# Sixteen experts on one core: rows of tokens by indirect DMA, a scatter matrix by comparison, and weights of two experts in one tile of 8 KB runs

## The chip, the cores and the metric

The kernel runs on one core of a Trainium2 chip: TensorE (PE; weight loads PEld), VectorE (DVE), ScalarE (ACT), GpSimd (POOL), and SyncE (SP), which here only issues transfers. Sixteen DMA engines move data between HBM and the on-chip memory. The metric is the device time of one execution in microseconds.

## What is computed

Two blocks of two layers each over 512 tokens of width 1024. The first block is attention and does not change. Each layer of the second block ends in a mixture of 16 experts, in which every expert takes the 64 tokens that score highest for it:

```python
def _ec_moe(h, router, w1, w3, w2):
    cap = EC_CAPACITY * n // N_EXPERTS          # 64
    probs = jax.nn.softmax(jnp.einsum('bnd,de->ben', h, router).astype(jnp.float32), axis=1)
    gates, idx = lax.top_k(probs, cap)
    xs = h[bidx, idx]
    a = jnp.einsum('becd,edf->becf', xs, w1)
    g = jnp.einsum('becd,edf->becf', xs, w3)
    y = jnp.einsum('becf,efd->becd', jax.nn.silu(a) * g, w2) * gates[..., None].astype(h.dtype)
    return jnp.zeros_like(h).at[bidx, idx].add(y)
```

All is fp32. One expert has three matrices of 1024 x 1024, 4 MB each; 16 experts make 201 MB a layer, each read once, and there are two such layers (0 and 1). Layer 0 follows a mixer, layer 1 a conformer.

## The kernel before

`moe(l)` (L1711) takes the experts in pairs, `p` from 0 to 7: the 64 tokens of one expert stand in columns 0 to 63 of TensorE's array, those of the other in 64 to 127. The residual `xn` is kept transposed, eight tiles of 128 features x 512 tokens; `kt` is the same, scaled, with tokens on the partitions.

**Routing.** Eight rounds of max and replace on DVE find each expert's tokens; a scan and two transposes turn that into `sT`, each token's slot in each expert.

**A pair.** `gather(p)` compares `sT` with the numbers 1 to 64 (`cst`) and gets a one-hot matrix `G` of tokens by slots. The tokens are gathered by TensorE: 32 matmuls of `kt` with `G` (L1780), four to each of eight feature chunks, whose results ACT and DVE scale and shift into `xs`. `slots` (L1788) gets the gates from `G` by four small matmuls and transposes `G` into `GT` by four more. `stage` (L1818) runs three times: `xs` by `w1`, `xs` by `w3`, and the product by `w2`; each is 32 matmuls (L1829) of 64 columns by 512, two of which, one for each expert, run side by side. An fp32 matmul runs in two passes, and the profile counts each pass, so it shows 64 in a stage and 64 in a gather; the prediction counts as the profile does. Between the second and the third the product is transposed (L1847). `scatter` (L1803) multiplies the result, split in a high and a low part, by `GT` (16 matmuls, L1807) and DVE adds the eight chunks to `xn` (L1808). The gather of pair p+1 is written after the scatter of pair p, and its chunks go between the matmuls of the first stage.

**Weights.** `load` (L1723) fetches a tile of 1 MB, 256 rows of one expert's matrix, as two runs of 4 KB in each of 128 partitions. There are 20 such tiles in turn, 12 (`mr`) and 8 (`mq`), 20 MB. 192 loads a layer stand on SP's queue in the order of use; each waits until the matmuls have done with the tile that it overwrites, and the first 20 are issued before the routing is done. Behind the last stand the conformer's first loads (L132, L134).

What sets the order is the code and a scheduler that places instructions of an engine by it; each engine runs its own list in order.

Of the kernel before, what the change touches and what calls it, by code (L numbers as in the profile page):

```python
# [22 lines left out]
KD = D // 128  # L23
# [4 lines left out]
SCRATCH = ((D, N), (2, 9, 128, 512), (1536, NT))  # L28
# [20 lines left out]
class K:  # L49
# [1510 lines left out]
    MB, MQ = 12, 8  # L1560
# [150 lines left out]
    def moe(self, l):  # L1711
# [5 lines left out]
        with self.ms, ExitStack() as es:  # L1717
            mp = es.enter_context(self.pool("moe"))
            W = (A["exp_w1"][l], A["exp_w3"][l], A["exp_w2"][l])
            todo = itertools.product(range(8), range(3), range(4), range(2))  # L1720
            order = itertools.cycle([(self.mring, "mr", self.MB)] * self.MB + [(mp, "mq", self.MQ)] * self.MQ)

            def load():  # L1723

                p, wi, kk, e = next(todo)
# [5 lines left out]
            kt = [self.t(mp, [128, D], tag=f"kt{t}") for t in range(4)]  # L1731
            gh = self.t(mp, [128, 8], tag="gh")
            sT = self.t(mp, [128, 4, E], tag="sT")
            with self.pool("mg") as gp:
                r, pr = self.route
                pt = self.bank()
                for t in range(4):
                    nc.tensor.transpose(pt[0:E, t * 128:t * 128 + 128], pr[:, t, :], self.ident[:])
                wk, cum = [self.t(gp, [E, N], tag=tag) for tag in ("wk", "cum")]
                pv = pt[0:E, :]  # L1740
                one = self.t(gp, [E, N], tag="mone")
                nc.gpsimd.memset(one[:], 1.0)

                for t in range(4):
                    for half in range(2):
                        pt = self.bank()
                        for c in range(4):
                            nc.tensor.transpose(pt[:, c * 128:c * 128 + 128], xn[4 * half + c][:, t * 128:t * 128 + 128],
                                                self.ident[:])
                        nc.scalar.activation(kt[t][:, half * 512:half * 512 + 512], pt[:], AF.Copy, scale=r[:, t:t + 1])  # L1750

                m8 = self.t(gp, [E, 8], tag="m8", bufs=2)
                for _ in range(CAP // 8):
                    nc.vector.max(m8[:], pv)  # L1754
                    nc.vector.match_replace(wk[:], m8[:], pv, -1.0)  # L1755
                    pv = wk[:]
                nc.vector.tensor_scalar(wk[:], wk[:], -1.0, None, op0=ALU.is_equal)
                nc.vector.tensor_tensor_scan(cum[:], one[:], wk[:], 0.0, op0=ALU.mult, op1=ALU.add)
                pts = []
                for x in (wk, cum):  # L1760
                    pt = self.bank()
                    for t in range(4):
                        nc.tensor.transpose(pt[:, t * 16:t * 16 + 16], x[:, t * 128:t * 128 + 128], self.ident[0:E, 0:E])
                    pts.append(pt[:, 0:64].rearrange("p (t e) -> p t e", t=4))
                nc.scalar.copy(sT[:], pts[0])
                nc.vector.tensor_tensor(sT[:], sT[:], pts[1], op=ALU.mult)
            xp = es.enter_context(self.pool("mx"))

            def gather(p):

                G = self.t(xp, [128, 512], tag="G", bufs=1)[:].rearrange("p (t n) -> p t n", t=4)
                nc.vector.tensor_tensor(G.rearrange("p t (e j) -> p t e j", e=2),  # L1772
                                        sT[:, :, 2 * p:2 * p + 2][:, :, :, None].to_broadcast([128, 4, 2, CAP]),
                                        cst[:][:, None, None, :].to_broadcast([128, 4, 2, CAP]), op=ALU.is_equal)
                xs = self.t(xp, [128, KD, 128], tag="xs", bufs=1)
                yield xs, G
                for c in range(KD):
                    px = self.bank()[:, 0:128]
                    for t in range(4):
                        mm(px, kt[t][:, c * 128:c * 128 + 128], G[:, t, :], start=t == 0, stop=t == 3)  # L1780
                    sc, sh = self.s1m[:, c:c + 1], mod[:, 24 + c, 0:1]
                    if c % 2 == 0:
                        nc.scalar.activation(xs[:, c, :], px, AF.Identity, scale=sc, bias=sh)  # L1783
                    else:
                        nc.vector.tensor_scalar(xs[:, c, :], px, sc, sh, op0=ALU.mult, op1=ALU.add)  # L1785
                    yield c

            def slots(p, G):  # L1788

                pg = self.bank()  # L1790
                for t in range(4):
                    mm(pg[:, 0:2], G[:, t, :], pr[:, t, 2 * p:2 * p + 2], start=t == 0, stop=t == 3)  # L1792
                for e in range(2):
                    es = slice(64 * e, 64 * e + 64)
                    nc.vector.tensor_scalar(gh[es, p:p + 1], pg[es, e:e + 1], 0.5, None, op0=ALU.mult)
                pb = self.bank()
                for t in range(4):
# [3 lines left out]
                return GT  # L1801

            def scatter(GT, yh, yl, st=None):  # L1803
# [8 lines left out]

            for p in range(8):
                parts = gather(p)
                xs, G = next(parts)
                next(parts)

                def stage(wi, lhs):  # L1818
                    ps = [self.bank(), self.bank()]
                    for kk in range(4):  # L1820
                        wt = []
                        for e in range(2):
                            wt.append(loaded.pop(0) if loaded else load())
                        for k2 in range(2):
                            k = 2 * kk + k2
                            next(parts, None)
                            for hf in range(2):
                                for e in range(2):
                                    mm(ps[hf][64 * e:64 * e + 64, :], lhs(k, e), wt[e][:, k2, hf * 512:hf * 512 + 512],  # L1829
                                       start=k == 0, stop=k == 7)  # L1830
                    return ps
                xl = lambda k, e: xs[:, k, 64 * e:64 * e + 64]
                pa = stage(0, xl)
# [5 lines left out]
                GT = slots(p, G)  # L1839
                pg = stage(1, xl)  # L1840
                sb = self.t(xp, [128, 8, 128], tag="xs", bufs=1)
                for hf in range(2):
# [3 lines left out]
                    for c in range(4):  # L1846
                        nc.tensor.transpose(pt[:, c * 128:c * 128 + 128], s[:, (4 * hf + c) * 128:(4 * hf + c + 1) * 128], self.ident[:])  # L1847
# [171 lines left out]
```

## Time and profile before

| | us |
|---|---|
| median of 3 runs (3161.67 to 3165.59) | 3161.85 |
| the profiled execution | 3164.56 |
| its span, first to last instruction | 3162.7 |
| TensorE busy in it | 2887.3 |
| DVE, ACT, GpSimd busy | 1503.0, 930.1, 799.7 |
| mean granted TensorE clock | 0.949 |
| expert loads (SP), `mr` and `mq` | 384 of 1024 KB |

The profile is of one execution, with times from the start of its span. Layer 0's experts run from about 1886 to 2402, layer 1's from about 2634 to 3150. A matmul's end is modelled, and neighbours overlap, so the step from one start to the next tells more than a busy time. The DMA share is the sum of all packets' times over 16 engines and can pass 1.

### The profile page before, as it was taken

Reading aid. Unit: us, or ns where it says so; the run is one execution under the profiler, and the core shown is the slowest. Engines: PE = TensorE matmul, PEld = TensorE weight load, DVE = VectorE, ACT = ScalarE, POOL = GpSimd, SP = SyncE. Lnnn points to the kernel's source line nnn. Section 1 sums busy time; section 2 is a strip of 40 time slices with the busy share of each in tenths; the row PEclk is TensorE's granted clock in tenths of the full one; section 3 lists DMA queues with packets and bytes.
Section 4 is the critical chain, followed back from the end, with each engine's and each line's share of the span. In section 5 each row is a group of like instructions: output and inputs, shape, how many; then the busy total and the mean of one; then the engine's idle time right before and its main releaser. Section 6 shows DMA issues by size and latency. Waiting matters only on the chain. (4 is left out here: it accounts for less than half of the span.)

```text
span 3162.7 us, 38266 instructions
## 1 busy us (share of the span) xinstructions
PE 2887.3 (91%) x14942; PEld 1846.0 (58%) x14942; DVE 1503.0 (48%) x2743; ACT 930.1 (29%) x1667; POOL 799.7 (25%) x669
## 2 busy tenths in 40 slices
PE   6889899998999999999998779998999998899988
PEld 3486577775688567765676754444445664444443
DVE  5886574556516555784366841112116552211122
ACT  2434344343424544344344221001002241001001
POOL 2242233422423334444344720000003330000000
PEclk8999899998899999999998889999999998999999
DMA  9631033221443134232322179999983557999993
GB/s 280 205 130 55 15 111 112 91 71 50 143 131 122 46 100 141 93 96 86 95 74 94 60 278 388 391 390 403 396 326 94 186 201 309 396 384 396 401 401 119
DMA packets 273924, 621.30 MB, mean 196 GB/s; under 512 B 15215, under 2 KB 144247, under 8 KB 273488
## 3 DMA queue, kind: packets, MB, share of 16 engines
q1 hardware_dynamic: 265568, 597.63, 52.1%
q0 software_dynamic: 4848, 17.04, 1.7%
q10 hardware_dynamic: 3328, 4.20, 0.4%
q8 instruction: 117, 1.92, 0.2%
q14 instruction: 63, 0.52, 0.1%
HBM read 603.96 MB, written 14.95 MB: 196 GB/s over the span
## 5 line engine op out<-in xcount | busy, mean ns | idle before, releaser
L154 POOL TENSOR_TENSOR wl<-ring,wh 128x512 fp32r<-128x512 f32 x304 | 418.2, 1379 | 655.0 <-ACT wh L153 636.9
L1829 PE MATMUL b<-mr,xs 128*64 128x512 f32 x1920 | 441.3, 605 | 0.0
L153 ACT CAST wh<-ring 128x512 fp32r<-128x512 f32 x304 | 186.9, 618 | 504.3 <-PE b L161 363.9
L159 PE MATMUL b<-hh,wh 128*128 128x512 f32 (+1 forms) x800 | 295.8, 371 | 3.0 <-DVE sc L621 3.0
L160 PE MATMUL b<-hh,wl 128*128 128x512 f32 (+1 forms) x800 | 291.6, 365 | 1.3 <-POOL wl L154 1.3
L161 PE MATMUL b<-hl,wh 128*128 128x512 f32 (+1 forms) x800 | 290.6, 365 | 0.1
L1829 PEld LDWEIGHTS b<-mr,xs 128*64 128x64 f32 x1920 | 143.7, 139 | 224.8 <-issue 214.7
L1829 PE MATMUL b<-mq,xs 128*64 128x512 f32 x1152 | 260.9, 600 | 0.0
L1780 PEld LDWEIGHTS b<-G,kt 128*128 128x128 f32 x1024 | 137.8, 212 | 136.1 <-issue 80.5
L1780 PE MATMUL b<-G,kt 128*128 128x128 f32 x1024 | 160.4, 309 | 52.1 <-DVE G L1772 52.1
L763 PE MATMUL av<-P,kv 128*64 128x512 f32 (+2 forms) x672 | 193.8, 522 | 2.9 <-ACT P L813 1.7
L1785 DVE TENSOR_SCALAR xs<-b,s1m,m 128x128 f32<-128x128 f32 x64 | 26.2, 409 | 322.2 <-PE b L1780 322.2
L159 PEld LDWEIGHTS b<-hh,wh 128*128 128x128 f32 x800 | 154.1, 193 | 32.3 <-issue 5.6
L160 PEld LDWEIGHTS b<-hh,wl 128*128 128x128 f32 x800 | 153.8, 192 | 27.0 <-issue 4.3
L161 PEld LDWEIGHTS b<-hl,wh 128*128 128x128 f32 x800 | 153.4, 192 | 25.1 <-issue 4.5
L1829 PEld LDWEIGHTS b<-mq,xs 128*64 128x64 f32 x1152 | 86.0, 138 | 138.0 <-issue 132.8
L813 ACT ACTIVATE P<-s 128x512 f32<-128x512 f32 (+2 forms) x224 | 116.6, 550 | 116.6 <-PE s L760 112.8
L362 PE MATMUL b<-wh,hh 128*128 128x256 f32 x512 | 148.9, 291 | 2.1 <-DVE kb L1160 1.3
L363 PE MATMUL b<-wl,hh 128*128 128x256 f32 x512 | 148.3, 290 | 0.3 <-POOL wl L154 0.3
L364 PE MATMUL b<-wh,hl 128*128 128x256 f32 x512 | 147.7, 289 | 0.4 <-DVE hl L345 0.4
L1855 DVE SCALAR_TENSOR_TENSOR yl<-b,gh,xs 128x512 fp32r<-128x512 f32 x32 | 22.6, 746 | 247.2 <-ACT xs L1854 247.2
L1783 ACT ACTIVATE xs<-b,m,s1m 128x128 f32<-128x128 f32 x64 | 29.3, 457 | 373.4 <-PE b L1780 373.4
(543 smaller groups left out, 5631.5 us busy)
## 6 DMA issues: line engine op xcount, KB each, us to landing
mr<-in_exp_w_dram SPq DMA_DIRECT2D x240, 1024.0 KB, 9.8
mq<-in_exp_w_dram SPq DMA_DIRECT2D x144, 1024.0 KB, 11.4
ring<-in_w_mod_dram SPq DMA_DIRECT2D x96, 512.0 KB, 4.2
ring<-in_w_in_dram SPq DMA_DIRECT2D x96, 512.0 KB, 3.7
ring<-in_ada_w_dram SPq DMA_DIRECT2D x48, 512.0 KB, 3.8
ring<-in_w_out_dram SPq DMA_DIRECT2D x32, 512.0 KB, 4.5
bias<-in_BS_dram POOLq DMA_DIRECT2D x16, 512.0 KB, 4.0
bias<-in_BT_dram POOLq DMA_DIRECT2D x16, 512.0 KB, 4.2
```

What stands on the lines that cost most here:

```text
L153: nc.scalar.copy(h, src)
L154: nc.gpsimd.tensor_tensor(l, src, h.bitcast(F32), op=ALU.subtract)
L159: m(out, w[0], x[0], start=start, stop=False, skip_group_check=chk)
L160: m(out, w[1], x[0], start=False, stop=False, skip_group_check=chk)
L161: m(out, w[0], x[1], start=False, stop=stop, skip_group_check=chk)
L362: m(o, hh, wh[:, kk, :], start=(k == 0 and i % 2 == 0), stop=False, skip_group_check=True)
L363: m(o, hh, wl[:, kk, :], start=False, stop=False, skip_group_check=True)
L364: m(o, hl, wh[:, kk, :], start=False, stop=stop, skip_group_check=True)
L763: mm(av[64 * i:64 * i + 64, a:b], vf(i, kt), P, start=start, stop=stop)
L813: nc.scalar.activation(p[:, :w], ps[:, :w], AF.Exp)
L1780: mm(px, kt[t][:, c * 128:c * 128 + 128], G[:, t, :], start=t == 0, stop=t == 3)
L1829: mm(ps[hf][64 * e:64 * e + 64, :], lhs(k, e), wt[e][:, k2, hf * 512:hf * 512 + 512], start=k == 0, stop=k == 7)
```

## The change

Four things are changed in `moe`, and the two constants for its tiles.

1. **Tokens.** The rows of `kt` are written to HBM scratch (`k_d`, four stores of 512 KB on ACT's queue). The slot matmul, now with four columns, also gives each slot's token number (`mnum` holds them), and GpSimd fetches the 128 rows of a pair by an indirect DMA into `xg`. TensorE transposes `xg` in eight pieces; ACT and DVE scale and shift as before. The 32 gather matmuls are gone.
2. **Scatter matrix.** `GT` is a comparison on DVE of the numbers 0 to 511 with the token numbers `gi`; the four transposes and ACT's copy are gone.
3. **Weights.** A tile is 2 MB, for both experts of a pair: 256 rows of each, and a partition holds two neighbouring rows of each, one run of 8 KB. `MB, MQ = 6, 4` keep 20 MB. 96 loads a layer. Because of that, feature k of a tile is every second one, hence `every2nd` and the scale vectors `sp1`, reordered by eight small matmuls.
4. **Order.** The scatter of pair p goes behind the first weight tile of pair p+1's first stage; the gather of pair p+1 is issued after the first stage of pair p and transposed inside its third.

The squares that close the layer go to `xg`, `xs` and one `mq` tile instead of `kt` and `G`.

```diff
-    MB, MQ = 12, 8
+    MB, MQ = 6, 4
...
-                w = self.t(pool, [128, 2, 1024], tag=tag, bufs=bufs)
-                nc.sync.dma_start(w[:], kview(W[wi][2 * p + e, kk * 256:(kk + 1) * 256, :]))
-                return w
+                w = self.t(pool, [128, 2, 2048], tag=tag, bufs=bufs)
+                nc.sync.dma_start(w[:], W[wi][2 * p:2 * p + 2, kk * 256:(kk + 1) * 256, :]
+                                  .rearrange("e (p k) n -> p e (k n)", k=2))
+                return w[:].rearrange("p e (k n) -> p e k n", k=2)
...
+                nc.scalar.dma_start(self.k_d[t * 128:t * 128 + 128, :], kt[:])
...
-                for c in range(KD):
-                    px = self.bank()[:, 0:128]
-                    for t in range(4):
-                        mm(px, kt[t][:, c * 128:c * 128 + 128], G[:, t, :], start=t == 0, stop=t == 3)
...
-                pb = self.bank()
-                for t in range(4):
-                    nc.tensor.transpose(pb[:, t * 128:t * 128 + 128], G[:, t, :], self.ident[:])
-                GT = self.t(xp, [128, N], F32R, tag="G", bufs=1)
-                nc.scalar.copy(GT[:], pb[:])
+                    mm(pg[:, 0:4], G[:, t, :], pg4[:, t, p, :], start=t == 0, stop=t == 3)
+                nc.vector.tensor_copy(ix[:, p:p + 1], pg[:, 2:3])
+                nc.vector.tensor_copy(gi[:, p:p + 1], pg[:, 2:3])
...
+                xg = self.t(xp, [128, D], tag="xg", bufs=1)
+                nc.gpsimd.indirect_dma_start(xg[:], None, self.k_d,
+                                             bass.IndirectOffsetOnAxis(ap=ix[:, p:p + 1], axis=0))
...
+                        nc.tensor.transpose(pt[:, k * 128:k * 128 + 128], every2nd(xg, k0 + k), self.ident[:])
...
+            def scatter(p, yh, yl, st=None):
+                GT = self.t(xp, [128, N], F32R, tag="GT", bufs=1)
+                nc.vector.tensor_scalar(GT[:], num[:, 0:N], gi[:, p:p + 1], None, op0=ALU.is_equal)
...
             for p in range(8):
+                xl = lambda k, e, xs=xs: xs[:, k, 64 * e:64 * e + 64]
+                pa = stage(xl, lambda kk: scatter(*late) if late and kk == 0 else None)
+                xg = gather(p + 1) if p < 7 else None
...
+                pg = stage(xl)
...
+                if p < 7:
+                    nxt = inputs(xg)
+                    xs = next(nxt)
+                py = stage(lambda k, e, sb=sb: sb[:, k, 64 * e:64 * e + 64],
+                           lambda kk: next(nxt, None) if kk in (1, 2) else None)
+                late = p, *outputs(p, py)
...
+            free = [self.t(xp, [128, D], tag=tag, bufs=1)[:] for tag in ("xg", "xs")]
+            free += [self.t(mp, [128, 4096], tag="mq", bufs=self.MQ)[:]]
```

TensorE's list where a pair's first stage begins, before: gather matmuls (`G`, `kt`) stand between the expert matmuls (`mr`).

```order
L1780 MATMUL b_16715<-G_16712,kt_3491_16105 128x128
L1780 MATMUL b_16715<-G_16712,kt_3492_16106 128x128
L1780 MATMUL b_16715<-G_16712,kt_3493_16107 128x128
L1780 MATMUL b_16715<-G_16712,kt_3494_16108 128x128
L1780 MATMUL b_16727<-G_16712,kt_3491_16105 128x128
L1780 MATMUL b_16727<-G_16712,kt_3492_16106 128x128
L1780 MATMUL b_16727<-G_16712,kt_3493_16107 128x128
L1780 MATMUL b_16727<-G_16712,kt_3494_16108 128x128
L1829 MATMUL b_16721<-mr_16723,xs_16714 64x512
L1829 MATMUL b_16721<-mr_16725,xs_16714 64x512
```

The same place after, from a third stage's last tile on: the expert matmuls of the next pair follow at once, and the scatter (`GT`) comes behind the first tile.

```order
L1859 MATMUL b_16986<-mq_17036,sb_16970 64x512 x2
L1859 MATMUL b_16987<-mq_17036,sb_16970 64x512 x2
L1859 MATMUL b_17052<-mq_17054,xs_16985 64x512 x2
L1859 MATMUL b_17053<-mq_17054,xs_16985 64x512 x2
L1859 MATMUL b_17052<-mq_17054,xs_16985 64x512 x2
L1859 MATMUL b_17053<-mq_17054,xs_16985 64x512 x2
L1844 MATMUL b_17066<-GT_17064,sb_17046 128x512
L1844 MATMUL b_17066<-GT_17064,yl_17047 128x512
```

GpSimd's list after the mixer's last split (`wl`): the number table, the copies for the slot matmul, and the gathers, in an engine that had nothing in this layer before.

```order
L154 TENSOR_TENSOR wl_15986<-ring_15967,wh_15985 128x512
L1739 DMA num_16093<-in_mnum_dram 128x516
L1773 COPY pg_3485_16092<-num_16093 128x32x2
L1772 COPY pg_3485_16092<-pr_16043 128x32x2
L1801 DMA xg_16213<-scratch,ix_16090 128x1024
L1801 DMA xg_16279<-scratch,ix_16090 128x1024
```

GpSimd now stands between the routing and the first expert matmul.

SP's list at the end of layer 0, after: the conformer's small load (`cv`) and its weights (`ring`).

```order
L182 DMA cv_3859_18069<-in_cv_dram 128x16
L132 DMA ring_18079<-in_cf_w_dram 128x4x128 x2
L132 DMA ring_18082<-in_cf_w_dram 128x4x128 x2
L134 DMA ring_18171<-in_w_mod_dram 128x4x256
L134 DMA ring_18173<-in_w_mod_dram 128x4x256
```

Before, the first two of these pairs of `ring` rows stood ahead of `cv`; now they stand behind it. The first `ring` load now waits for the squares' last sum (L317), whose operands lie where that ring tile will be; before, it waited for expert matmuls of the last pair.

## Rows read from the trace of the kernel before

**Rows 1.** waits of SP, 1900 to 2350 us: total us, times, longest.
```profile
SPq L1728 <- PE b L1829: 340.7, 85, 13.6
```

**Rows 2.** waits of TensorE's weight loads, same stretch: the one wait for a transfer.
```profile
PEld b L1829 <- DMA mr<-in_exp_w_dram: 0.2, 1, 0.2
```

**Rows 3.** busy us of each engine by stretch, then granted clock, DMA share, GB/s.
```profile
1880.00:1886.00 6.00, 1.16 (x9) 1.04 (x9) 4.74 (x10) 0.21 (x1) 0.00 (x0) 0.50 1.03 410
1960.00:1980.00 20.00, 20.00 (x108) 9.31 (x110) 2.92 (x7) 2.69 (x5) 0.00 (x0) 1.00 0.97 353
2120.00:2150.00 30.00, 25.43 (x128) 12.97 (x126) 9.14 (x14) 3.35 (x6) 0.00 (x0) 1.00 1.03 410
```

**Rows 4.** chain that ended last, one expert pair of layer 0: start, us, what.
```profile
2146.53 1.87 PE b L1829 x8
...
2169.33 13.95 PE b L1829 x64
2184.70 13.95 PE b L1829 x64
2199.46 1.44 PE b L1807 x5
2200.92 2.53 DVE xn L1808 x4
...
2206.93 3.09 PE b L1780 x16
2210.03 2.43 PE b L1829 x8
```

**Rows 5.** groups by line, layer 0, gather: busy us, mean ns, idle before.
```profile
L1780 PE MATMUL b<-G,kt 128*128 128x128 f32 x512 | 80.1, 308 | 26.0 <-DVE G L1772 26.0
```

**Rows 6.** timeline of TensorE, last pair of layer 1; columns: start, us.
```profile
3105.90 1.05 PE L1792 MATMUL b<-pr,G 128*128 128x2 f32 x8
...
3107.38 7.09 PE L1829 MATMUL b<-mq,xs 128*64 128x512 f32 x32
...
3122.75 14.01 PE L1829 MATMUL b<-mr,xs 128*64 128x512 f32 x64
```

**Rows 7.** DMA, 2120 to 2150 us, runs of 4 KB: packets, MB, share.
```profile
DMA packets 3187, 12.29 MB, mean 410 GB/s; under 512 B 190, under 2 KB 190, under 8 KB 3186
...
q1 hardware_dynamic: 3186, 12.27, 102.5%
```

**Rows 8.** DMA, 12 to 15.3 us: a load with 8 KB runs, almost alone.
```profile
DMA packets 109, 0.84 MB, mean 253 GB/s; under 512 B 7, under 2 KB 7, under 8 KB 7
...
q1 hardware_dynamic: 109, 0.84, 60.1%
```

**Rows 9.** timeline of TensorE where the first pair of layer 0 begins.
```profile
1885.99 3.76 PE L1780 MATMUL b<-G,kt 128*128 128x128 f32 x16 [1.20 <-DVE G L1772]
1889.67 2.22 PE L1829 MATMUL b<-mr,xs 128*64 128x512 f32 x8
```

**Rows 10.** timeline of SP: the first load that waited for a freed tile.
```profile
1894.87 6.79 SPq L1728 DMA_DIRECT2D mr<-in_exp_w_dram  x4
```

**Rows 11.** timeline of TensorE: first expert matmul of layer 1.
```profile
2637.49 2.07 PE L1829 MATMUL b<-mr,xs 128*64 128x512 f32 x8
```

**Rows 12.** tile bias, 512 KB loads issued by GpSimd: issue ns (min/median/max), landing.
```profile
L1023 POOL DMA_DIRECT2D bias<-in_BS_dram x16: 528/568/604, 167.6 to 1280.7; - x16
...
DMA to landing us min/median/max: 3.7/4.0/6.1
```

**Rows 13.** timeline of TensorE where layer 0 ends and the conformer begins.
```profile
2384.71 4.51 PE L1829 MATMUL b<-mr,xs 128*64 128x512 f32 x20
...
2400.97 1.05 PE L317 MATMUL b<-mean,G 128*128 128x2 f32 x8 [0.78 <-DVE G L283]
...
2408.07 0.80 PE L159 MATMUL b<-eh,wh 128*128 128x512 f32 x1 [1.59 <-ACT eh L344]
```

**Rows 14.** timeline of SP: the conformer's first weight loads.
```profile
2353.79 14.09 SPq L132 DMA_DIRECT2D ring<-in_cf_w_dram  x4
```

More of the change, by code (lines that the diff above doesn't have):

```diff
@@ L1730, in moe @@
             loaded = [load() for _ in range(self.MB + self.MQ)]
[L1731 to L1735, printed above, removed]
+            xp = es.enter_context(self.pool("mx"))
+            gh, gi = [self.t(xp, [128, 8], tag=tag) for tag in ("gh", "gi")]
+            ix = self.t(xp, [128, 8], I32, tag="ix")
@@ L1739, in moe @@
[L1739 to L1742, printed above, removed]
-                for t in range(4):
[L1745 to L1750, printed above, removed]
@@ new lines, in moe @@
+            nc.gpsimd.tensor_copy(pg4[:, :, :, 2:4], num[:, 512:516][:, :, None, None].to_broadcast([128, 4, 8, 2]))
+            pp = self.bank()
+            sp1 = self.t(xp, [128, 2, 8], tag="sp1")
+            for i, src in enumerate((self.s1m[:], mod[:, 24:32, 0])):
+                for h in range(2):
+                    for par in range(2):
+                        o = 8 * i + par
+                        mm(pp[64 * h:64 * h + 64, o:o + 7:2], self.ident[:, par:par + 127:2], src[:, h:8:2],
+                           start=True, stop=True)
@@ new lines, in inputs @@
+            def inputs(xg):
+                xs = self.t(xp, [128, KD, 128], tag="xs", bufs=1)
+                yield xs
+                for k0 in (0, 4):
+                    pt = self.bank()
+                    for k in range(4):
+                        nc.tensor.transpose(pt[:, k * 128:k * 128 + 128], every2nd(xg, k0 + k), self.ident[:])
+                    for i in range(4):
+                        k = k0 + i
+                        px, sc, sh = pt[:, i * 128:i * 128 + 128], sp1[:, 0, k:k + 1], sp1[:, 1, k:k + 1]
+                        if k % 2 == 0:
+                            nc.scalar.activation(xs[:, k, :], px, AF.Identity, scale=sc, bias=sh)
+                        else:
+                            nc.vector.tensor_scalar(xs[:, k, :], px, sc, sh, op0=ALU.mult, op1=ALU.add)
+                    yield k0
@@ L1811, in scatter, with stage @@
                         st(c, xn[c][:])
-            for p in range(8):
[L1814 to L1833, printed above, removed]
+            def stage(lhs, between=None):
+                ps = [self.bank(), self.bank()]
+                for kk in range(4):
+                    wt = loaded.pop(0) if loaded else load()
+                    for k2 in range(2):
+                        k = 2 * kk + k2
+                        for hf in range(2):
+                            for e in range(2):
+                                mm(ps[hf][64 * e:64 * e + 64, :], lhs(k, e), wt[:, e, k2, hf * 512:hf * 512 + 512],
+                                   start=k == 0, stop=k == 7)
+                    if between:
+                        between(kk)
+                return ps
+            nxt = inputs(gather(0))
+            xs = next(nxt)
+            for _ in nxt:
+                pass
+            late = None
+            for p in range(8):
+                xl = lambda k, e, xs=xs: xs[:, k, 64 * e:64 * e + 64]
+                pa = stage(xl, lambda kk: scatter(*late) if late and kk == 0 else None)
+                xg = gather(p + 1) if p < 7 else None
                 s = self.t(xp, [128, 1024], tag="yl", bufs=1)
@@ L1994 @@
     k = K(ctx, tc, A, out)
-    k.x_d, k.kf_d, k.u_d = scratch
+    k.x_d, k.kf_d, k.u_d, k.k_d = scratch
     k.setup()
```

114 lines of the change are left out of this document (59 added, 55 removed).

## The prediction

> **What bounds the kernel now.** I read the waits in the expert stages first. SP, which issues the weight loads, stands 340.7 of 450 us waiting for matmuls to free a tile [rows 1]; TensorE waits for a load for 0.2 us in all [rows 2]. So TensorE is the bound. The busy time by stretch then says how far behind the transfers are, and here it is not far: where the queue is full it moves 410 GB/s with a DMA share of 1.03, and in a stretch where TensorE is busy for 20.00 of 20 us it moves 353 GB/s with a share of 0.97 already [rows 3]. Last, the chain through one pair: it starts at 2146.53 and the next at 2210.03, 63.5 us. Of that, three times 13.95 are the expert matmuls of the stages; the rest is gather, a gap of 1.42 before the third stage, one of 0.81 behind it, and 7.5 us of scatter (2199.46 to 2206.93) in which TensorE mostly waits for DVE [rows 4]. A pair's weights are 24 MB, 25.17 million bytes: at 410 GB/s 61.4 us. Two bounds lie 2 us apart, and the change lowers one far more than the other.
>
> **TensorE's work in a pair.** Removed: the gather. The 512 passes of a layer, at 308 ns each, overlap, and are busy for 80.1 us, so 10.0 a pair [rows 5]. The four transposes of `G` go too: `slots` stands for 3107.38 - 3105.90 = 1.48 us on TensorE, of which the eight passes of the slot matmuls are busy for 1.05 [rows 6], so some 0.5 for the transposes. So does the gap of 0.81, because the next pair's matmuls stand behind the third stage at once. The exposed scatter of 7.5 us becomes 16 matmuls within the first stage. Their cost lies between 16 x 0.218 = 3.5 us, the step from one expert matmul of as many columns to the next (13.95 / 64), and DVE's own pace, 8 x 0.63 = 5.1 (2.53 for four, [rows 4]); the five matmuls that took 1.44 us lie between (16 x 0.29 = 4.6, with a start in it), and I take 4.3. What is added: eight transposes of `xg`, at the 0.5 us of four in `slots` 1.0 us if the rows are there, and up to 1.4 where they wait for a scaled chunk. Sum: 41.85 + 4.3 + 1.42 + 1.0 for the slot matmuls + 1.0 = 49.6, near 50 us, with 48 as the low end and, if a scatter waits as it does now, 41.85 + 1.42 + 7.5 + 1.05 + 1.4 = 53.2 as the high one.
>
> **The gather's own path.** It is issued after the first stage and wanted in the third. Between them lie 13.95 us of second stage. GpSimd's issue and landing have no row for an indirect transfer; the nearest are 512 KB loads that GpSimd issues: 0.57 us and 3.7 to 6.1 [rows 12]. Even twice that is hidden in the second stage. The price is not the wait but 0.524 MB more on the queue. DVE's comparison and the copies lie beside matmuls, since DVE is busy for only 9.14 of 30 us there [rows 3]. If this cover were gone, a whole landing, some 6 us a pair, would stand on TensorE; but TensorE will wait for weights longer than that (below), so the end would move little.
>
> **The loads become the bound.** At 50 us of TensorE a pair, weights would have to come at 25.17 / 50 = 503 GB/s, which no row shows. So the step that sets the end is the queue's rate with runs of 8 KB. Two rows price it. With runs of 4 KB, 3186 packets filled 102.5% of 16 engines for 30 us: 410 / 1.025 = 400 GB/s per unit of share [rows 7]. With runs of 8 KB, 0.84 MB filled 60.1% of 3.3 us at 253 GB/s: 253 / 0.601 = 421 [rows 8]. A packet of double size takes less than double time. At a share of 1 that is 421, at the share of 1.025 that the full queue shows it is 431, and if nothing is won it stays at 410. I take 420, because the short row has an almost idle chip around it. A pair then takes (25.17 + 0.52) / 0.420 = 61.2 us, 11 us more than TensorE needs.
>
> The Trainium skill speaks against this part: "DMA: Bandwidth & Descriptors", section "Latency and other measured facts", reports that transfers are slow when the rows of neighbouring partitions lie a large power of two apart, 207 GB/s at 512 KiB and 103 at 4 MiB. In the old tile only the two runs of one partition lie 512 KB apart, and 410 GB/s came, so the trace does not show the rule reaching that far; the new distance of 4 MB is shown by no row, and at 207 GB/s the sum below would have 889 us of loads in place of 438.
>
> **The start.** The first expert matmul now waits for the first gather. `G` is ready at 1885.99, when the first gather matmul starts [rows 9]. Then: slot matmuls 0.6 and cast 0.2, issue 0.6 and landing 3.7 to 6.1 [rows 12], four transposes 0.7 and scaling 0.5 (estimates, from the 0.5 us of four at full clock above and from DVE's 2.92 us for seven instructions, [rows 3]). The first expert matmul at 1889.67 [rows 9] becomes one at 1894 (1892 to 1898), 4.3 us later; this is the price of the moved wait, and GpSimd, which has nothing else in this layer, queues nothing behind it but the copies. The first reload of a tile, at 1894.87 before [rows 10], comes after the 16 matmuls of a larger tile, and eight took 2.22 us at the start, where the clock is low [rows 9]: all of them at 1.2 GHz, twice 3.5, make 7 us, so 1901, and first bytes at 1903.
>
> **The sum.** The first ten tiles are there. 86 tiles of 2.097 MB and seven gathers of 0.524 remain, 184.0 MB, at 420 GB/s 438 us: 1903 + 438 = 2341. The last 16 matmuls add 3.5: 2344.6. Before, they ended at 2384.71 + 4.51 = 2389.22 [rows 13]. Layer 0 gains 44.6. Layer 1 starts at 2637.49 [rows 11] and ends its last matmuls at 3122.75 + 14.01 = 3136.76 [rows 6]; the same working gives 44.4. Off this go 1 us for the conformer's first weight load and 1 us for the clock. That load waited for expert matmuls and was issued by 2353.79 [rows 14], long before its use at 2408.07 [rows 13]; now it waits for the squares' sum, which is at 2400.97 and so 11.75 us behind the last expert matmul [rows 13]. Counted from that matmul, sum, landing and split take 17.4 to 19.5 us where 18.85 are free (2408.07 less 2389.22): 0 to 1 us, 3 at most. Behind this load on SP stand only the conformer's other weights.
>
> So 87 us: the profiled execution of 3164.56 becomes 3077.6, and since it lies 2.7 us over the median of 3161.85, the median becomes 3075. Each 10 GB/s is worth some 10 us a layer at this place: 410 gives 3096, 432 gives 3051. With 432 and the better ends of the start it is 3048.
>
> **Rivals.** *Long runs bring nothing or lose a little.* The queue keeps 395 to 410 GB/s. The row with a full queue [rows 7] is for it, the shorter time per byte of [rows 8] against it. 410: 184.0 / 0.410 = 449 us, 3096; 395: 466 us, 3131. In this case the change doesn't do what its third part says, and lives off the other parts.
>
> *The clock falls.* TensorE will now wait about 1.5 us behind each of its 3.5 us of a tile, and waiting has cost clock: in 1880 to 1886, where it was busy for 1.16 of 6 us, the granted clock was 0.50, so 1.2 GHz in place of 2.4; at 20 of 20 and at 25.43 of 30 us busy it was 1.00 [rows 3]. The new duty, about 0.8, is close to the second of these. If the clock were low half the time, a pair would take 50 / 0.75 = 66.7 us in place of 61.2, for the 3.3 pairs that are paced by loads: 18 us a layer, 3111.
>
> The Trainium skill, "TensorE: Matmul & The Clock Gate", section "HAM oscillation — how this bites in real kernels", tells of just this: a group of matmuls shorter than the wait for its load starts cold each time. Here the group is longer than its wait, so by that rule the loss stays away; its chance below rests on the rows.
>
> *The queue is faster.* At 432 to 440 GB/s loads take 426 to 418 us: 3050 to 3035. TensorE's 50 us a pair end only at about 2305, so it is not in the way.
>
> *The other side: the new tile slows the queue.* One partition takes two runs from two experts, whose matrices lie 4 MB apart, where before they lay 512 KB apart in one matrix; each instruction also covers twice the bytes. If that costs rate, the loads set the end and every per cent counts. The point from which it decides: 184.0 MB in the 2389.2 - 3.5 - 1903 = 482.7 us that there are now, 381 GB/s. At the lowest rate in the rows, 353 [rows 3], loads take 521 us, 83 more than in the sum, and the time is 3241. For it speaks that no row shows such a pitch; against it, that the old pitch cost nothing.
>
> **How the numbers follow.** Forecast, 413 to 430 GB/s: 0.60, own range 3055 to 3092. Long runs bring nothing: 0.17 (3092 to 3131). Clock: 0.08 (3111, with a tail). Faster queue: 0.07 (3035 to 3050). Slower queue: 0.08 (3150 to 3241). The predicted time is 3075. For 8 in 10 the range must hold the forecast and two thirds of the first two rivals; low 3048, high 3110. A measurement can tell about 0.2%, 6.3 us, from no change; only a rate between 379 and 383 GB/s falls in that band, so same is 0.02, slower 0.08, faster 0.90.
>
> **What would show it.** In the profile after: TensorE's weight loads wait for `mr` and `mq` transfers, by about 11 us a pair from some 2145 on, and none before; SP still waits for matmuls to free a tile, but with the other nine under way, so that the queue never runs dry; the rate between 1950 and 2330 stands at 420 GB/s with a share over 1.0; first expert matmul at 1894; last one at 2345; no matmul waits for `xg` except the first pair's; granted clock 1.00 in these stretches. I am wrong if the rate is under 410 or over 432, if the granted clock falls under 0.9 in the second half of the layer, or if TensorE waits for DVE in the scatter, so that its pair passes 61 us.

## The result and the profile after

The changed kernel takes 3082.44 us (median of 4 runs, 3079.57 to 3084.68), the kernel before 3161.76: the ratio is 0.9747, 95% interval 0.973 to 0.9764. Forecast were 3075 and a range of 3048 to 3110. The profiled execution took 3082.83 us, with a span of 3080.8, where the sum gave 3077.6.

The waits answer to [rows 1] and [rows 2]. First SP's longest group from 1900 to 2350 us, then what TensorE's weight loads and its matmuls waited for from 1890 to 2350 (total us, times, longest):

```profile
SPq L1728 <- PE b L1859: 221.0, 66, 21.0
```

```profile
PEld b L1859 <- DMA mr<-in_exp_w_dram: 24.4, 20, 2.2
PEld b L1859 <- DMA mq<-in_exp_w_dram: 18.0, 12, 2.2
```

```profile
PE b L1859 <- DMA mr<-in_exp_w_dram: 23.0, 16, 2.3
PE b L1859 <- DMA mq<-in_exp_w_dram: 15.1, 12, 2.3
...
PE b L1817 <- DMA xg<-scratch,ix: 7.1, 1, 7.1
```

The weight loads' 0.2 us of waiting for transfers has become 42, and the matmuls stand for 7.1 us behind the first gather and behind no other. SP still waits, but with the other tiles' loads under way: the bound has passed from TensorE to the loads. The windows answer to [rows 3] (busy us and count of PE, PEld, DVE, ACT, POOL; granted clock, DMA share, GB/s):

```profile
1900.00:1950.00 50.00, 49.88 (x236) 18.71 (x233) 8.13 (x18) 5.48 (x10) 0.96 (x1) 1.00 0.94 384
1950.00:2000.00 50.00, 49.89 (x236) 20.03 (x235) 13.27 (x26) 5.47 (x10) 0.95 (x1) 1.00 1.01 420
...
2100.00:2150.00 50.00, 43.15 (x190) 16.93 (x192) 11.04 (x20) 3.64 (x6) 0.95 (x1) 0.97 1.01 421
2150.00:2200.00 50.00, 41.13 (x184) 15.87 (x182) 11.31 (x22) 4.30 (x8) 0.95 (x1) 0.97 1.01 420
```

The rate stands at 420 or 421 GB/s wherever the queue is full, in the half in which TensorE hardly stops as in the half in which it waits. TensorE's timeline shows both (start, us, idle before): where the first pair starts, where the second follows it, one pair later on, and the end of layer 0.

```profile
1883.57 0.57 PE L1768 MATMUL b<-ident,GT 16*128 16x16 f32 x4 [6.75 <-DVE GT L1762]
...
1887.33 1.84 PE L1794 MATMUL b<-pg,G 128*128 128x4 f32 x8 [0.96 <-DVE G L1789]
1896.29 1.95 PE L1817 MATMUL b<-ident,xg 128*128 128x128 f32 x8 [7.12 <-DMA xg<-scratch,ix]
1898.17 14.59 PE L1859 MATMUL b<-mr,xs 128*64 128x512 f32 x64
...
1944.54 3.60 PE L1859 MATMUL b<-mr,xs 128*64 128x512 f32 x16
1948.07 0.50 PE L1844 MATMUL b<-GT,sb 128*128 128x512 f32 x1
...
1951.92 8.38 PE L1859 MATMUL b<-mr,xs 128*64 128x512 f32 x38
```

```profile
2105.91 3.65 PE L1859 MATMUL b<-mq,xs 128*64 128x512 f32 x16 [1.41 <-ACT sb L1833]
...
2153.43 3.65 PE L1859 MATMUL b<-mq,sb 128*64 128x512 f32 x16 [1.53 <-DMA mq<-in_exp_w_dram]
2158.49 3.65 PE L1859 MATMUL b<-mq,sb 128*64 128x512 f32 x16 [1.41 <-DMA mq<-in_exp_w_dram]
2163.38 3.65 PE L1859 MATMUL b<-mq,sb 128*64 128x512 f32 x16 [1.23 <-DMA mq<-in_exp_w_dram]
```

```profile
2345.09 3.65 PE L1859 MATMUL b<-mr,sb 128*64 128x512 f32 x16 [1.24 <-DMA mr<-in_exp_w_dram]
...
2360.58 1.05 PE L317 MATMUL b<-mean,mq 128*128 128x2 f32 x8 [0.84 <-DVE mq L283]
...
2367.70 0.80 PE L159 MATMUL b<-eh,wh 128*128 128x512 f32 x1 [1.59 <-ACT eh L344]
```

The first pair takes 1944.54 - 1898.17 = 46.4 us without a scatter; the next two, with a scatter inside of 3.85 us (1948.07 to 1951.92), start 49.3 and 51.1 apart. The four after that are 60.9, 62.5, 61.0 and 61.0. There a tile's 3.65 us are mostly followed by a wait of 1.2 to 1.5 us for the next tile, and once a pair, behind the tiles that follow the scatter, by one of 2.0 to 2.3 us. The last expert matmul ends at 2348.74, 40.5 us earlier than before [rows 13]; layer 1's ends 81.9 us earlier than in [rows 6]:

```profile
3051.26 3.65 PE L1859 MATMUL b<-mr,sb 128*64 128x512 f32 x16 [1.23 <-DMA mr<-in_exp_w_dram]
```

For the experiments one length is of use: from the first transposes behind the routing (1883.57 here, 1882.89 before) to the end of the last expert matmul.

```profile
1882.89 0.58 PE L1763 MATMUL b<-ident,wk 16*128 16x16 f32 x4 [7.59 <-DVE wk L1757]
```

It leaves out what the stages ahead of it differ by (the first transposes lie between 1877.6 and 1885.9 in the runs below). The two layers of one kernel agree in it within about 2 us, 3 for e1c and 4 for e1. In layer 0 it is 506.3 before and 465.2 after.

### The profile page after: what moved, and what is told of

It is laid out like the page before. It is cut to its first block, busy times and chain, and to the rows that moved or that the text cites. A ratio compares the mean times of both kernels' runs of the same rounds, so it can differ in the third digit from the quotient of the medians.

```text
span 3080.8 us, 36122 instructions
## 1 busy us (share of the span) xinstructions
PE 2760.5 (90%) x14014; PEld 1717.2 (56%) x14014; DVE 1514.0 (49%) x2793; ACT 923.3 (30%) x1651; POOL 815.7 (26%) x689
## 4 chain that ended last, share of the span: by engine, by line
PE 28%; DMA 19%; DVE 5%; POOL 2%; ACT 2%; issue 1%; SPq 0%; DVEq 0%; ACTq 0%; POOLq 0%
DMA mr<-in_exp_w_dram 10%; PE b L1859 10%; DMA mq<-in_exp_w_dram 8%; PE b L159 4%; PE b L161 4%; PE b L160 3%; PE av L763 1%; PE b L209 1%; PE b L1844 1%; PE q L275 1%; DVE lh L1262 0%; PE s L757 0%; DMA scratch<-sb 0%; PE b L324 0%; DVE f L1473 0%
## 5 line engine op out<-in xcount | busy, mean ns | idle before, releaser
L1859 PE MATMUL b<-mr,xs 128*64 128x512 f32 x1216 | 283.7, 617 | 37.2 <-DMA mr<-in_exp_w_dram 28.7
L1859 PE MATMUL b<-mq,xs 128*64 128x512 f32 x832 | 189.2, 604 | 25.2 <-DMA mq<-in_exp_w_dram 16.8
L1859 PEld LDWEIGHTS b<-mr,xs 128*64 128x64 f32 x1216 | 90.1, 141 | 216.6 <-issue 154.6
L1801 POOL DMA_INDIRECT xg<-scratch,ix x16 | 15.5, 967 | 728.0 <-DVE ix L1795 687.5
L1859 PE MATMUL b<-mr,sb 128*64 128x512 f32 x704 | 159.4, 597 | 18.5 <-DMA mr<-in_exp_w_dram 18.3
L1883 DVE TENSOR_TENSOR yl<-yl,b 128x512 f32<-128x512 f32 x32 | 22.0, 688 | 254.1 <-PE b L1859 254.1
L1859 PEld LDWEIGHTS b<-mq,xs 128*64 128x64 f32 x832 | 60.2, 138 | 146.2 <-issue 101.6
L776 POOL TENSOR_TENSOR acc<-acc,P 128x256 f32<-128x256 f32 (+2 forms) x96 | 99.5, 1039 | 118.2 <-ACT P L813 94.2
L757 PE MATMUL s<-q1l,k 128*128 128x512 f32 (+2 forms) x288 | 113.2, 403 | 2.1 <-DVE sc L802 1.6
```

The costliest lines, as they stand in the source:

```text
L757: mm(ps, k1[i][:, kt * 128:kt * 128 + 128], q1[i][:, a:b], start=True, stop=False)
L1859: mm(ps[hf][64 * e:64 * e + 64, :], lhs(k, e), wt[:, e, k2, hf * 512:hf * 512 + 512], start=k == 0, stop=k == 7)
```

## Experiments

Each ran in 4 executions (10 for the one on the kernel before), beside the kernel before on the same chip. The time is the median; ratios are to the kernel before, with their interval. The ratio of two experiments is uncertain by about 7 us; where the question is smaller, the length above decides.

| kernel | us | ratio | layer 0, length above |
|---|---|---|---|
| before | 3161.76 | 1 | 506.3 |
| changed | 3082.44 | 0.9747 (0.973 to 0.9764) | 465.2 |
| e1, runs of 4 KB | 3104.46 | 0.9806 (0.9789 to 0.9823) | 479.2 |
| e1c, 8 KB, 1 MB an instruction | 3082.74 | 0.9739 (0.9723 to 0.9755) | 467.2 |
| e2, before with 8 KB | 3171.68 | 1.0022 (1.0008 to 1.0036) | 508.1 |
| e3, later gathers left out | 3065.30 | 0.9682 (0.9665 to 0.9699) | 456.2 |
| e4, scatter exposed | 3082.45 | 0.9744 (0.9727 to 0.976) | 466.2 |
| e5, first gather left out | 3070.39 | 0.9698 (0.9682 to 0.9715) | 458.3 |
| e6, runs of 16 KB | 3067.08 | 0.9694 (0.9678 to 0.9711) | 459.1 |
| e7, all gathers on TensorE | 3074.90 | 0.9715 (0.9699 to 0.9731) | 462.1 |
| e8, first gather on TensorE | 3080.49 | 0.9734 (0.9716 to 0.9752) | 462.9 |
| e9, 16 KB, weights in place | 3083.56 | 0.974 (0.9724 to 0.9756) | 464.9 |
| e11, two gathers by DMA | 3078.46 | 0.9729 (0.9713 to 0.9745) | 462.5 |

### Is it the length of a run that sets the rate?

**e1: runs of 4 KB.**

```diff
-                nc.sync.dma_start(w[:], W[wi][2 * p:2 * p + 2, kk * 256:(kk + 1) * 256, :]
-                                  .rearrange("e (p k) n -> p e (k n)", k=2))
+                for e in range(2):
+                    nc.sync.dma_start(w[:, e], W[wi][2 * p + e, kk * 256:(kk + 1) * 256, :]
+                                      .rearrange("(k p) n -> p k n", k=2))
...
```

> The changed kernel, with each weight tile fetched as before in runs of 4 KB (two transfers of 1 MB for a tile, 512 KB between the two runs of a partition) and the features taken in their old order. Theory, the queue sets the end and long runs give its rate: the rate falls from 420 to 410 GB/s, so 184.0 MB take 449 us in place of 438, 11 us more a layer, 3104 us. Rival, the rate comes from a queue that is always full and not from the runs: it stays at 420 GB/s and the time at 3082.

**e1c: runs of 8 KB, two instructions.** The same loop over `e`, with `"(p k) n -> p (k n)"`.

> The changed kernel with runs of 8 KB, but two transfers of 1 MB for each tile, one for each expert, so that no instruction reads two places 4 MB apart and each moves as many bytes as before. Theory, only the length of a run counts: 420 GB/s, 3082 us. Rival, the bytes of an instruction or the distance of 4 MB count: the rate moves towards 410 GB/s (3104 us), or up over 425 (under 3072).

**e6: runs of 16 KB.**

```diff
-                nc.sync.dma_start(w[:], W[wi][2 * p:2 * p + 2, kk * 256:(kk + 1) * 256, :]
-                                  .rearrange("e (p k) n -> p e (k n)", k=2))
+                nc.sync.dma_start(w[:].rearrange("p e n -> p (e n)"),
+                                  W[wi][2 * p + kk // 2, kk % 2 * 512:kk % 2 * 512 + 512, :]
+                                  .rearrange("(p k) n -> p (k n)", k=4))
```

> The changed kernel with runs of 16 KB: a tile takes 512 rows of one expert, four to a partition (the weights then stand in the wrong places of the tile, so the product is another one; the bytes and the matmuls are the same). Theory, each run has a fixed part: from 1/410 at 4 KB and 1/420 at 8 KB follows 1/425 at 16 KB, so 433 us in place of 438, 5 us less a layer, 3072 us. Rival, packets end at 8 KB, and nothing is won: 3082, 420 GB/s.

The same window, 2120 to 2150 us, of e1, the changed kernel, e1c and e6 in this order (columns as above):

```profile
2120.00:2150.00 30.00, 27.57 (x112) 10.15 (x112) 4.88 (x11) 1.20 (x2) 0.95 (x1) 1.00 1.03 409
```

```profile
2120.00:2150.00 30.00, 25.41 (x110) 8.88 (x108) 2.75 (x4) 2.37 (x4) 0.00 (x0) 0.94 1.01 421
```

```profile
2120.00:2150.00 30.00, 28.21 (x117) 10.73 (x114) 3.70 (x8) 1.82 (x4) 0.95 (x1) 1.00 1.01 419
```

```profile
2120.00:2150.00 30.00, 23.88 (x112) 8.70 (x112) 3.53 (x7) 3.00 (x6) 0.00 (x0) 1.00 1.01 427
```

All four queues are full; what differs is the run: 409 GB/s at 4 KB, 420 at 8, 427 at 16. 22 us between e1 and the changed kernel were expected and 22 measured; by the length, 14.0 in layer 0 and 11.2 in layer 1, where 11 were expected. Bytes of an instruction and the distance of 4 MB between a partition's two runs (e1c halves the one and has no such distance) change nothing, at least together. In e1 the runs are shorter and also lie 512 KB apart in pairs; no run parts the two, but that 16 KB gain again speaks for the length. The 16 KB gave 15 us where 10 were expected; the layer is 6.1 us shorter where 5 were expected, and the rate is 427 in place of the 425 worked out, so the rest lies within what a measurement can tell.

### Is it the runs alone?

**e2: the kernel before, with the new tile only.**

> The kernel before with the new weight tile alone (2 MB for both experts, runs of 8 KB, every second feature); tokens are gathered by TensorE, the scatter stays where it was. Theory, TensorE is the bound there and waits for no load: 3162 us, within 6 us, while the queue shows 420 GB/s where it is full. Rival, the loads were a hidden part of the bound of before: 3130 us or less.

It took 0.2% more (0.08 to 0.36%), and its layer 508.1 us in place of 506.3. The new load alone is worth nothing, since TensorE was the bound; the rival falls. Yet its queue is as much faster as in the changed kernel: in a stretch in which it is full it moves 424 GB/s, the kernel before 409 (columns as above, e2 first).

```profile
2180.00:2200.00 20.00, 19.05 (x89) 7.82 (x86) 3.82 (x6) 2.44 (x4) 0.00 (x0) 1.00 1.01 424
```

```profile
2180.00:2200.00 20.00, 18.98 (x90) 8.08 (x87) 1.94 (x3) 2.44 (x4) 0.00 (x0) 1.00 1.03 409
```

The extra 0.2% may lie on TensorE: in layer 0 the gather's matmuls and the product's transposes, which now read every second column, are busy for 81.6 and 11.9 us in place of 80.1 and 10.5. That was not tested by itself.

### What do the later gathers cost?

**e3: later gathers left out.**

```diff
+                if p:
+                    return self.xg0
-                xg = self.t(xp, [128, D], tag="xg", bufs=1)
+                xg = self.xg0 = self.t(xp, [128, D], tag="xg", bufs=1)
```

> The changed kernel without the seven later gathers of a layer: all pairs use the rows that the first one fetched, so that part of the computation is left out. Theory, gathers share the engines with the weights and cost their bytes, 7 x 0.524 MB at 420 GB/s, 8.7 us a layer: 3065 us. Rival, they ride on a queue of their own beside the weights and cost nothing: 3082.

3065.3, and 9.0 us a layer: seven gathers cost what their bytes cost on a full queue. They are hidden as a wait and paid as bytes, as the prediction had it.

### Is the place of the scatter worth anything?

**e4: scatter exposed.**

```diff
                 late = p, *outputs(p, py)
+                if p < 7:
+                    scatter(*late)
```

and the first stage runs without it.

> The changed kernel with the scatter back behind each pair's third stage, where the next pair's matmuls wait for it. Theory, TensorE has 11 us a pair to spare once the lead of loads is used up, and the exposed scatter costs it some 4 to 5 us more a pair: hidden, 3082 to 3086 us. Rival, what stands on TensorE between two pairs stops the freeing of tiles and so the queue, as long as the queue sets the end: 4 us for each of 14 pairs, some 3138 us.

TensorE around the end of a pair, from its timeline:

```profile
2153.23 3.65 PE L1859 MATMUL b<-mq,sb 128*64 128x512 f32 x16 [2.65 <-DMA mq<-in_exp_w_dram]
2158.10 3.65 PE L1859 MATMUL b<-mq,sb 128*64 128x512 f32 x16 [1.22 <-DMA mq<-in_exp_w_dram]
2162.61 1.20 PE L1844 MATMUL b<-GT,sb 128*128 128x512 f32 x4 [0.85 <-ACT sb L1833]
...
2166.46 3.65 PE L1859 MATMUL b<-mr,xs 128*64 128x512 f32 x16
```

3082.45: no difference. While the scatter stands (2162.61 to 2166.46) loads go on, at 422 GB/s from 2160 to 2167, and the next tile starts without a wait for one. The rival, that it would stop the queue, falls.

### What does the start cost?

**e5: first gather left out.**

```diff
...
+                if p == 0:
+                    return k0t
                 xg = self.t(xp, [128, D], tag="xg", bufs=1)
                 nc.gpsimd.indirect_dma_start(...)
```

> The changed kernel without the first gather of a layer: the first pair takes the first 128 tokens, which still stand on the chip, so that part of the computation is left out; the transposes and all else stay. Theory, the 7 us for which the first expert matmul waits for that transfer delay the first freed tile, the queue and the end one for one: 7 us less a layer, 3068 us; and the version in which TensorE gathered the first pair gained only 2 us because its gather stood between the first matmuls and freed a tile in 6 us in place of 3.5. Rival, the start is not what sets the end: 3080 to 3082.

**e8: first gather on TensorE.** `first` gathers by 32 matmuls, as the kernel before does, four ahead of each pair of feature chunks:

```diff
+                for k in range(8):
+                    px = self.bank()[:, 0:128]
+                    for t in range(4):
+                        mm(px, every2nd(kts[t], k), G[:, t, :], start=t == 0, stop=t == 3)
...
```

> The changed kernel in which the first pair of a layer alone is gathered by TensorE, its matmuls between those of the first stage, so that no expert matmul waits for an indirect transfer; the seven others stay. Theory, while the loads set the end, the time at which the first tile is freed sets it one for one: first expert matmul at 1890 in place of 1898, first reload at 1895 to 1897 in place of 1902.5, 6 to 7 us less a layer, 3068 to 3070 us. Rival, the queue starts with the stores of the rows still under way, or TensorE gives the start back: 3082.

First reloads on SP (start, us from first to last issue), in the changed kernel, e5 and e8, whose routing transposes start at 1883.57, 1883.73 and 1880.03:

```profile
1902.50 0.37 SPq L1728 DMA_DIRECT2D mr<-in_exp_w_dram  x1
```

```profile
1895.59 7.23 SPq L1728 DMA_DIRECT2D mr<-in_exp_w_dram  x3
```

```profile
1893.95 17.12 SPq L1728 DMA_DIRECT2D mr<-in_exp_w_dram  x4
```

In e5 the first reload comes 7.1 us earlier after the routing, and the layer is 6.9 us shorter: one for one. The measured time fell by 12 us, 14 were expected. In e8 it comes 5.0 us earlier, but the layer gains 2.3 and the time 2 in place of 12 to 14: that expectation failed. Three reloads in e5 stand 3.4 us apart, those of e8 5.6 ((17.12 - 0.37) / 3), because the gather's matmuls stand between those of the tile. A tile of 2.097 MB takes a queue of 420 GB/s 5.0 us, so loads were short at first: e8's queue moved 336 GB/s from 1895 to 1910, which leaves 3.0 us of loads undone, where e5's moved 429 from 1900 to 1910.

```profile
1895.00:1910.00 15.00, 15.00 (x79) 7.05 (x80) 1.83 (x4) 1.06 (x3) 0.00 (x0) 1.00 0.96 336
```

```profile
1900.00:1910.00 10.00, 10.00 (x52) 3.85 (x50) 2.42 (x7) 1.19 (x2) 1.03 (x1) 1.00 1.02 429
```

5.0 us earlier less 3.0 is near the 2.3 that the layer gained. What counts is not the first freed tile but the first few.

### Was the indirect gather needed?

**e7: all gathers on TensorE**, in the third stage, with all else of the change, and three `mq` tiles in place of four.

```diff
-    MB, MQ = 6, 4
+    MB, MQ = 6, 3
...
-                nc.gpsimd.indirect_dma_start(...)
-                return xg
+                return G
...
+                        mm(px, every2nd(kts[t], k), xg[:, t, :], start=t == 0, stop=t == 3)
```

> The changed kernel with the tokens gathered by TensorE again (no rows to HBM, no indirect transfers), the gather's matmuls between those of the third stage; scatter matrix by comparison, place of the scatter and runs of 8 KB stay. The rows kept on the chip cost one tile: three mq in place of four. Theory, TensorE is then the bound again: 50 us a pair less 1.4 for the transposes plus 8.7 for the gather make 57.5, the start is 8 us earlier, and layer 0 ends at 1890 + 8 x 57.5 - 4 = 2346 in place of 2349: about 3077 us. Rival, loads still set the end, and only their bytes and the start count: 182.4 MB from 1897 on, 13 us less a layer, 3056 us. Third, matmuls and loads hinder each other when both are near the bound: over 3090.

3074.9 us where 3077 were expected, and 3.1 us a layer less than the changed kernel: the fastest complete version here, if only by 0.25%, with intervals that just meet. TensorE is the bound in it, but only just (window of e7, columns as above):

```profile
2200.00:2300.00 100.00, 99.77 (x513) 45.23 (x510) 18.39 (x34) 10.92 (x20) 0.00 (x0) 1.00 1.01 420
```

TensorE is busy for 99.77 of 100 us and the queue is full at 420 GB/s. Five pairs in a row start exactly 57.0 us apart (57.5 had been worked out), where the bytes of a pair alone want 25.17 / 0.420 = 59.9; the lead of loads pays the difference, and it lasts to the end of the layer.

**e11: e7, with the rows of pairs 1 and 2 by indirect transfer.**

```diff
+                if p not in (1, 2):
+                    return G
...
```

> The version with all gathers on TensorE, but with the rows of pairs 1 and 2 fetched by indirect transfers, while the lead of loads lasts and TensorE is the bound. Theory, TensorE does 2 x 7 us less, after which the loads set the end: first bytes at 1898, 183.5 MB at 420 GB/s and the last tile make 2339 in place of 2343, 4 us less a layer, 3067 us. Rival, with all on TensorE the loads were the bound already, and a gather more on the queue costs its bytes: 3078.

3078.46, 462.5 us a layer as in e7: the expectation of 4 us less a layer failed. Its window:

```profile
2200.00:2300.00 100.00, 96.18 (x490) 45.14 (x492) 20.24 (x37) 9.73 (x18) 0.00 (x0) 1.00 1.01 420
```

TensorE now waits for loads while their rate is the same. What was taken from it came back as that wait, and the loads ended no earlier than TensorE's work does in e7. The time on record for the rival, 3078, is what came. Its reason, that loads were the bound in e7 already, does not fit e7's window, in which TensorE is busy for 99.77 of 100 us.

I had reckoned with a full queue from the first load on. The first reload came as in e7 (15.0 us after the routing, there 14.9), but the first tiles are freed slowly, as in e8, and the queue moved 373 GB/s from 1905 to 1925:

```profile
1905.00:1925.00 20.00, 20.00 (x103) 8.73 (x104) 3.84 (x10) 2.11 (x4) 1.04 (x1) 1.00 0.97 373
```

That is 2.2 us of loads. Where the other 2 us of the miss lie was not looked into.

### Would longer runs help the whole kernel?

**e9: 16 KB, with the weights in place.** A tile is 512 rows of one expert, and the features of a tile are every fourth.

```diff
-            todo = itertools.product(range(8), range(3), range(4))
+            todo = itertools.product(range(8), range(3), range(2), range(2))
...
-                a = k // 2 * 256 + k % 2
-                return x[:, a:a + 255:2]
+                a = k // 4 * 512 + k % 4
+                return x[:, a:a + 509:4]
```

> The changed kernel with runs of 16 KB and weights where they belong: a tile is 512 rows of one expert, every fourth feature belongs to one place, and the reordering of the scale vectors (32 small matmuls) stands ahead of the rounds on DVE. Theory, the rate of 427 GB/s that such runs showed is worth 7 us a layer, but two tiles are freed together after 7 us in place of one after 3.6, at the start and at the end: 6 to 7 us a layer are lost again, 3079 to 3083 us. Rival, the size that is freed at once does not matter: 3067.

3083.56 with 427 GB/s in its full stretches: the 15 us that the rate gave in e6 are gone. Its first reload and its last expert matmuls (routing transposes at 1880.85):

```profile
1902.75 0.80 SPq L1728 DMA_DIRECT2D mr<-in_exp_w_dram  x2
```

```profile
2338.65 7.08 PE L1860 MATMUL b<-mr,sb 128*64 128x512 f32 x28 [2.27 <-DMA mr<-in_exp_w_dram]
```

The first reload comes 21.9 us after the routing in place of 18.9, and at the end two tiles' matmuls, 7.1 us, follow the last load instead of one's 3.65. Together that is 6.4 us, and the layer is 5.8 longer than e6's. A larger unit of freeing takes back what a longer run gives.

## Why the prediction was right, point by point

**TensorE's work in a pair.** Worked out 49.6 with a scatter, measured 49.3 and 51.1, without a scatter 46.4. The scatter in line took 3.85 us, between its bounds of 3.5 and 5.1.

**The loads become the bound.** The step on which the sum rests, 420 GB/s, was the rate measured; e1 and e2 show that it is the runs, and that they count only once TensorE's work is shorter. The rows gave 410 to 431, so that the 420 picked between them is right to the unit is luck in part. Pairs stand mostly 61.0 apart where 61.2 were forecast. The matmuls waited 38 us for loads in layer 0, from about 2040 on and not from 2145, 7.6 a pair for the last five, where 11 were worked out for three. Here the prediction counted back from the end. By its own terms, ten tiles ahead, 4.13 us for TensorE to use one (49.6 / 12) and 5.1 for the queue to load one (61.2 / 12), the lead is gone by some 2060.

The rule of the Trainium skill, "DMA: Bandwidth & Descriptors", section "Latency and other measured facts", is on rows of neighbouring partitions that lie a large power of two apart, which no run here has. For the two runs of one partition the runs show no such loss: 420 GB/s with 4 MB between them, 419 in e1c without.

**The start: a term sized wrongly, in two places that mostly cancel.** The first expert matmul came at 1898.17, not at 1894 (its own upper bound was 1898). From the chain, the last store of the rows and the first gather, and from GpSimd's timeline the gather's issue:

```profile
1877.86 13.10 DMA scratch<-sb
...
1891.81 4.34 DMA xg<-scratch,ix
```

```profile
1891.81 1.03 POOL L1801 DMA_INDIRECT xg<-scratch,ix  x1 [20.76 <-DMA scratch<-sb]
```

The issue alone takes 1.03 us where 0.57 was taken from direct loads. But issue and landing together were priced rightly: from the end of the store at 1890.96 to the landing at 1896.15 it is 5.2 us, where 0.6 and 3.7 to 6.1 were taken. Three other things cost more.

- `G` was used at 1887.33 and not at 1885.99 (0.7 us of that is this execution's later routing), and the slot matmuls took 1.84 us at a granted clock of 0.50 where 0.6 were taken.
- The gather was ready at 1889.4 and waited until 1890.96 for the last store of the rows, issued on ACT's queue at 1877.86: it took 13.1 us to land beside a queue full of weights. That store was named as an edit, but the sum had no term for it. Not all of this wait is lost: in e1c the gather began 1.5 us earlier after the routing, beside weight loads, and took 6.65 us to land.
- All eight transposes, and not four, stood before the first expert matmul, at the low clock: with the scaling 2.0 us from the landing on, where 1.2 were taken.

Against this, the first reload followed 4.3 us after the first matmul and not 7: the granted clock was 0.50 until 1898 and 1.00 from 1900 on. So the reload came at 1902.50 where 1901 was worked out. That the sum comes out so near in spite of the late matmul is luck, owed to this second error.

**The sum.** Loads filled the queue from 1905, 2 us later than in the sum, and the last landed at 2345.05 (2341), after 440 us in place of 438. Layer 0 gained 40.5 us (44.6), layer 1 41.4 (44.4). e5 shows that each us at the start is one at the end. The 2 us taken off were not needed: squares and the conformer's first matmul follow the last expert matmul by 11.8 and 19.0 us, and before it was 11.75 and 18.85 [rows 13]. So the gain of 81.9 is 5 us short of the 87. Another 2 us of the miss of 7.4 lie in the median: the profiled execution of before lay 2.7 over its median, that of after 0.4.

**Rivals.** Long runs bring nothing: then the changed kernel would take what e1 takes, 3104, and it does not. A slower queue: no window of the changed kernel with a full queue shows one. A falling clock: it fell, but where it cost nothing. Behind waits of 1.2 to 1.5 us it stayed at 1.00. Behind the one wait of 2.0 to 2.3 us in each of four pairs it fell to about 0.5 for a few microseconds, so that the 32 matmuls there took 8.7 to 8.8 us in place of 7.09; the windows of 50 us in this half therefore show 0.97 or 1.00. One of the four:

```profile
2128.00:2130.00 2.00, 2.00 (x8) 0.71 (x6) 0.00 (x0) 0.00 (x0) 0.00 (x0) 0.55 1.03 430
```

```profile
2127.30 8.79 PE L1859 MATMUL b<-mr,xs 128*64 128x512 f32 x32 [2.25 <-DMA mr<-in_exp_w_dram]
2136.99 3.65 PE L1859 MATMUL b<-mr,xs 128*64 128x512 f32 x16 [0.90 <-DMA mr<-in_exp_w_dram]
```

The next matmuls still waited 0.9 to 1.1 us for their load each time, so nothing was lost. The prediction had named 1.00 throughout. The length of the wait alone does not decide it: in e4 a wait of 2.65 us (above, at 2153.23) left the clock at 1.00. The Trainium skill's "TensorE: Matmul & The Clock Gate", section "HAM oscillation — how this bites in real kernels", tells of groups of matmuls shorter than the wait for their load, which start cold each time. No group here is shorter than its wait, so this trace does not show its case. That a longer group keeps the loss away, as the prediction read it, held behind the short waits, but not behind those of 2.0 to 2.3 us, with 7.09 us of matmuls just ahead of the wait and as many behind it.

**What the parts are worth.** Not the prediction's question, but the runs answer it. With runs of 8 KB and a bound of about 60 us a pair by loads, TensorE had to fall below that. Taking the gather from it does so while the scatter stays exposed (e4: 466.2), and moving the scatter does so while the gather stays on TensorE, there in the third stage (e7: 462.1); the scatter matrix by comparison is in both and was not tested alone. The two together gain nothing over one, and against e7 the indirect transfer costs 3 us a layer; e3 and e5 price its bytes and its start.

## What to carry to other kernels

When TensorE stands a few per cent above the transfers, price a cut of its work by the rate of a full queue and not by what is removed: of some 14 us a pair taken from TensorE here, 2.5 were left where loads set the pace, and the rest came while a lead of loads lasted. Once the queue sets the end, four things counted here: its bytes, its rate, the time at which the first few buffers are freed, and the work that follows the last load; where the scatter stood did not. And a gather on TensorE, which just had the time for it, was 3 us a layer cheaper than one on the full queue.

## What the runs showed of the hardware

- A full queue moved 409, 420 and 427 GB/s with runs of 4, 8 and 16 KB, and, at 8 KB, 419 to 421 with 1 MB or 2 MB to an instruction.
- The last of four stores of 512 KB on ACT's queue took 13.1 us to land beside the weight loads, where 512 KB loads by GpSimd took 3.7 to 6.1 us [rows 12].
- An indirect gather of 128 rows of 4 KB landed in 4.3 us on an idle queue and in 8.6 to 10.1 us beside a full one; its issue took 0.95 to 1.03 us (layer 0 of the changed kernel).
- TensorE's granted clock stayed at 1.00 behind waits of 1.2 to 1.5 us between groups of 3.65 us, fell to about 0.5 behind four waits of 2.0 to 2.3 us, and stayed at 1.00 behind one of 2.65 us in e4.
